# First expert gather from full-precision rows, and four more early weight loads

## Chip, cores and metric

The kernel runs on one core of one Trainium2 chip. The metric is device time in microseconds from one execution; lower is better. The traced execution is one of its own, beside three timed runs.

## What is computed

The reference is one layer of a hybrid encoder trunk on 512 tokens of 1024 channels, float32 in and out:

```python
proj = x @ w_in                       # q,k,v of two attentions, two gate logits
y_sb = stick_breaking(...) @ w_br_sb
y_ca = chunked_relpos(...) @ w_br_ca
mixed = (sigmoid(gl_sb + b0) * y_sb + sigmoid(gl_ca + b1) * y_ca) @ w_out
x = layer_norm(ALPHA * x + mixed, ln1_g, ln1_b)
# router: best of 4 groups, then the best 2 of its 8 experts, with weights
for each expert e: hid = silu(x @ w_gate[e]) * (x @ w_up[e]); y += weight * hid @ w_down[e]
return layer_norm(ALPHA * x + y, ln2_g, ln2_b)
```

The kernel computes an expert only for the tokens that chose it: 32 experts with 64 slots each, two experts to a pair. A dense version behind a branch takes over if an expert overflows; it does not run here.

## The kernel before

**Stages.** Projections and both attentions fill the first 345 us or so. Then comes the output projection `out_proj(half, tt)` (line 748), over two halves of 512 output columns and four token tiles `tt` of 128 rows; VectorE adds its result to the residual rows `hp[tt]` (line 762). With the second half of a tile its first layer norm and its routing follow, spread over the products of later tiles by the table `todo` (lines 1043 to 1053): keys are (half, tile, step), and entries past the last tile are run from `TAIL` (lines 1083 to 1089) together with the first gathers and some filler products that only keep TensorE busy. Then the experts run, `gate_up(e)`, `down(e)`, `act(e)`, in an order written out by hand, and `finish()` adds, normalizes and stores the rows.

**Routing.** `route(tt)` picks group and experts on VectorE; its rank product `rk` (lines 915 to 919) gives each token its slot, from which `slots_of` builds `onehot[:, tt, :]` (lines 928 and 929, 256 columns: the slots of experts 0 to 3). `finish_routing()` makes the row numbers for the rest.

**The first gather.** The tokens of experts 0 to 3 don't come by DMA but by TensorE: for each of the eight channel blocks `c`, `first_x(c, ts)` multiplies 128 columns of the normed rows (stationary) with `onehot[:, tt, :]` (moving) and adds up over the four tiles, through `gathered` (line 995). To do that with fp32r operands the normed rows are split into two parts: `split_h(tt)` (line 837) normalizes `hp[tt]` in two halves on VectorE (line 848), copies each to an fp32r tile `hh` on ACT (line 112), and subtracts it from the row on POOL to get `hl` (line 115). So there are 8 x 4 x 2 = 64 matmuls. Then it stores the rows to DRAM, `hD` (line 853), from where later experts' tokens are fetched with indirect DMA.

**Weights.** An expert's weights come as six chunks of 512 KB, `we0` to `we191`, each loaded by `raw_load()` (line 1063) into a buffer chosen by the table `RING`: `slots` (20 buffers), `slots2` (15), `hip` (4), `lop` (4), 43 in all, used again in turn. `slots2` also holds two gate tiles `gca`, `hp[0..3]`, the rows `lng` and `lnb` of the norm's parameters, and the eight tiles `hh`, `hl`. `load_early` (line 1072) asks for the first 13 chunks at (0,0,5): eight in `slots`, `K2` = 5 in `slots2`. All others are asked for when the experts begin, up to 47 ahead of use, but the queue order is a scheduler's: it issues a load on SP as soon as its buffer is expected to be free, between the stores to `hD`. SP's queue is then fixed, and each entry waits for its own buffer.

Of the kernel before, what the change touches and what calls it, by code (L numbers as in the profile page):

```python
# [9 lines left out]
F32 = mybir.dt.float32  # L10
F32R = mybir.dt.float32r
# [3 lines left out]
AF = mybir.ActivationFunctionType  # L15
OP = mybir.AluOpType
AX = mybir.AxisListType

P = 128
S = 512  # L20
D = 1024
C = D // P
TT = S // P
# [19 lines left out]
WARM = 10  # L43
XEB = 4
AHEAD = 47
EARLY = 13
K2 = 5
EARLY_AT = (0, 0, 5)
NL = 40
PT = (1, 4, 10, 5)  # L50
RA = 2
# [14 lines left out]
IDLE_LAST = 6  # L66

K_POOL = ((0, 1), (0, 2), (0, 3), (1, 0), (1, 1), (1, 2), (1, 3))
H_POOL = (0, 1, 2, 3)
LATE_C = (2, 3)  # L70
H_STT = (0, 1, 2, 3)

LAST_RING = [1 if j % 4 == 1 else 0 for j in range(43)]
RING = [0] * 8 + [1] * K2 + [0] * 12 + [2] * 4 + [3] * 4 + [1] * (NSLOT2 - K2)
SCB = 2
# [28 lines left out]
def trunk(ctx, tc, xT, x, wm, wv, wbr, wout, wr, br, bg, rbx, lnp, lncol, wexp, out):  # L104
    nc = tc.nc
# [3 lines left out]
    def split(hi, lo, src, scale=None, eng=None, fix=False):  # L109

        if scale is None:
            act = nc.scalar.activation(hi, src, AF.Copy)  # L112
            pin(act, fix)
            held[1] = act
            pin((eng or nc.vector).tensor_sub(lo, src, hi.bitcast(F32)), fix == "both")  # L115
        else:
            pin(nc.scalar.activation(hi, src, AF.Copy, scale=scale), fix)
            pin(nc.vector.scalar_tensor_tensor(
                out=lo, in0=src, scalar=scale, in1=hi.bitcast(F32), op0=OP.mult, op1=OP.subtract
            ))  # L120

    in_order = [False]
    held = [None, None]

    def pin(ins, fix=True):
        if in_order[0] and fix:
            tc.keep_in_program_order(ins)

    def mm(ps, a, b, start, stop):
        pin(nc.tensor.matmul(ps, a, b, start=start, stop=stop))  # L130
# [30 lines left out]
    def slot(shape, dtype, name, pool=None):  # L161
        return (pool or slots).tile(shape, dtype, tag="slot", name=name)
# [104 lines left out]
    for cc in range(4):  # L267
        t = slot([P, 2, S], F32, f"xraw{cc}")
        h = slot([P, 2, S], F32R, f"xh{cc}")
        lo = slot([P, 2, S], F32R, f"xl{cc}")  # L270
# [15 lines left out]
    for k in range(4):  # L286
        t = slot([P, 2, S], F32, f"part{k}")
# [8 lines left out]
    for k, pack in enumerate(PACKS[:3]):  # L296
        m = ap_.tile([P, S], BF16, name=f"mask{k}")
        nc.gpsimd.memset(m, 1.0)
        for _, i, off in pack:
            blk = m[:, off + 128 * i : off + 128 * i + 128]  # L300
            nc.gpsimd.affine_select(
                out=blk, in_=blk, pattern=[[-1, P]], compare_op=OP.is_gt, fill=0.0, base=0, channel_multiplier=1
# [160 lines left out]
    def scores(b, p, pack):  # L463
        q, k = QKT["q", b, p], QKT["k", b, p]
        ps = pp.tile([P, S], F32, tag="sc", name="sc", bufs=SCB)
        for h, i, off in pack:
            n = P * (i + 1)
            for z in range(2):
                mm(ps[:, off : off + n], q[:, h, 0, i * P : (i + 1) * P], k[:, h, z, :n], z == 0, z == 1)
        return ps  # L470
# [99 lines left out]
    def run(g, n=1000):  # L570
        if g is None:
            return None
        for _ in range(n):
            try:
                next(g)
            except StopIteration:
                return None
        return g
# [13 lines left out]
    for b in range(2):  # L592
        for p in range(4):
# [6 lines left out]
            for k, pack in enumerate(PACKS):  # L600
# [3 lines left out]
                ps = scores(b, p, pack)  # L604
# [15 lines left out]
    slots2 = es_w.enter_context(tc.tile_pool(name="slots2", bufs=NSLOT2, reuse_waits="tile"))  # L620
# [96 lines left out]
    for t in xgb:  # L717
        nc.gpsimd.memset(t, 0.0)
    onehot = keep.tile([P, TT, 4 * CAP], F32R, name="onehot")
# [17 lines left out]
        out=tri, in_=ones, pattern=[[1, P]], compare_op=OP.is_gt, fill=0.0, base=0, channel_multiplier=-1  # L737
# [6 lines left out]
    hp = [slot([P, D], F32, f"hp{t}", slots2) for t in range(TT)]  # L744
# [83 lines left out]

        return ap.unsqueeze(len(ap.shape)).to_broadcast(list(ap.shape) + [n])

    hh, hl = [None] * TT, [None] * TT
    V = nc.vector

    def centre(tt, mean):
        nc.vector.scalar_tensor_tensor(out=hp[tt], in0=hp[tt], scalar=mean, in1=lng, op0=OP.subtract, op1=OP.mult)

    def split_h(tt):

        r, mean = rs[tt]
        if tt in LATE_C:  # L840
            centre(tt, mean)
        t = slot([P, D], F32R, f"hh{tt}", slots2)
        lo = slot([P, D], F32R, f"hl{tt}", slots2)
        for k in range(2):
            cs = slice(k * S, (k + 1) * S)
            src = hp[tt][:, cs]
            if tt in H_STT:
                nc.vector.scalar_tensor_tensor(out=src, in0=src, scalar=r, in1=lnb[:, cs], op0=OP.mult, op1=OP.add)
            else:
                pin(nc.scalar.activation(src, src, AF.Copy, scale=r))  # L850
                nc.gpsimd.tensor_add(src, src, lnb[:, cs])
            split(t[:, cs], lo[:, cs], src, eng=nc.gpsimd if tt in H_POOL else None, fix=tt in H_STT)
        nc.sync.dma_start(hD[tt * P : (tt + 1) * P, :], hp[tt])
        hh[tt], hl[tt] = t, lo

    NBUF = dict(sc=2, tr=3, pj=2, av=1)
    hqs = [spare.tile([P, 4, P]) for _ in range(2)]
# [23 lines left out]
    def scale1(tt):  # L881
        r, mean = rstd(tail, lnst[tt], TT, None if tt in LATE_C else lambda mean: centre(tt, mean))
        u = small([P, 1], f"u{tt}")
        V.scalar_tensor_tensor(out=u, in0=mean, scalar=-1.0, in1=r, op0=OP.mult, op1=OP.mult)
        rs[tt] = r, mean
        base[tt] = small([P, NL], f"base{tt}")
        V.scalar_tensor_tensor(out=base[tt], in0=swr, scalar=u, in1=brb, op0=OP.mult, op1=OP.add)
        V.scalar_tensor_tensor(out=base[tt], in0=plg[tt][0], scalar=r, in1=base[tt], op0=OP.mult, op1=OP.add)
# [106 lines left out]
    def gathered(ps, c, ts):  # L995

        for tt in ts:
            for n, h in enumerate((hh, hl)):
                mm(
                    ps, h[tt][:, c * P : (c + 1) * P], onehot[:, tt, :],  # L1000
                    tt == 0 and n == 0, tt == TT - 1 and n == 1,
                )

    def xtile(g, j):
        if (g, j) not in xe:
# [5 lines left out]
    def first_x(c, ts):  # L1011

        if len(first) <= c:
            t = (["pj"] * 2 + ["tr"] * 3 + ["av", "sc", "pj"])[c]
            first.append(pp.tile([P, 4 * CAP], F32, tag=t, name="trf", bufs=NBUF[t]))
        gathered(first[c], c, ts)
# [4 lines left out]
    lnb = slot([P, D], F32, "lnb", slots2)  # L1021
# [6 lines left out]
    def turn(tt, q):  # L1028
        lg[tt, q] = logits(tt, q)
        next(lg[tt, q])  # L1030

    def first_half(tt):
        lnst[tt] = stats(tail, hp[tt], 0)

    def begin(tt):
        stats(tail, hp[tt], 1, lnst[tt])

    def choose(tt):
        run(lg[tt, 1])
        rt[tt] = route(tt)  # L1040
        next(rt[tt])

    todo = {}
    for at, half in ((0, 0, 0), 0), ((0, 0, 1), 0), ((0, 0, 3), 0), ((0, 3, 2), 1), ((0, 3, 4), 1), ((0, 3, 6), 1), ((1, 0, 0), 1):
        todo[at] = [lambda half=half: wo[half].append(stream.get())]
    for tt in range(TT):
        at = (0, tt + 1) if tt + 1 < TT else (1, 0)
        todo.setdefault((*at, PT[0]), []).extend([lambda tt=tt: turn(tt, 0), lambda tt=tt: first_half(tt)])
        todo.setdefault((*at, PT[1]), []).append(lambda tt=tt: run(lg[tt, 0]))
        todo.setdefault((1, tt + 1, PT[0]), []).extend([lambda tt=tt: turn(tt, 1), lambda tt=tt: begin(tt), lambda tt=tt: scale1(tt)])  # L1050
        todo.setdefault((1, tt + 1, PT[1]), []).extend([lambda tt=tt: choose(tt)])
        todo.setdefault((1, tt + 1 + PT[2] // 8, PT[2] % 8), []).append(lambda tt=tt: run(rt[tt]))
        todo.setdefault((1, tt + 1 + PT[3] // 8, PT[3] % 8), []).append(lambda tt=tt: split_h(tt))

    seq = []
    for e in range(NE):
# [6 lines left out]
    def raw_load():  # L1063
        i = n_raw[0]
        n_raw[0] += 1
        n = len(RING)
        pool, tag = rooms[RING[i % n] if i < len(seq) - n else LAST_RING[i - len(seq) + n]]
        t = pool.tile([P, D], F32, tag=tag, name=f"we{i}")
        nc.sync.dma_start(t, wexp[seq[i]])
        raw_e.append(t)  # L1070

    def load_early():
        for _ in range(EARLY):
            raw_load()

    todo.setdefault(EARLY_AT, []).append(load_early)
    for half in range(2):
        for tt in range(TT):
            for k, _ in enumerate(out_proj(half, tt)):
# [422 lines left out]
```

## Time and profile before

| | us |
|---|---|
| runs | 679.63, 677.06, 679.90; median 679.63 |
| profiled execution | 682.24, its span 680.4 |
| mean granted TensorE clock | 0.987 |
| PE busy, of the span | 640.9 (94%) |
| DVE busy | 408.2 (60%) |
| ACT busy | 322.6 (47%) |
| POOL busy | 105.1 (15%) |
| DMA moved | 158.62 MB, mean 233 GB/s |

The page of the profile gives busy times by engine, the span in 40 slices of about 17 us, the chain of work that ended last (followed back from the last instruction, at each step to what released it), and the costliest groups of instructions. A row of a timeline has the start, the length, the engine, the line in the kernel, the operation and its tiles; in square brackets stands how long the engine was idle before it and who ended that. "PE" is TensorE, "DVE" VectorE, "ACT" ScalarE, "POOL" GpSimd, "SPq" the queue of SyncE, which issues DMAs. Matmul lengths are modelled with their pipeline, so successive ones overlap, and their rate is read from their starts. A busy PE is not the same as a PE at its peak: fillers count as busy.

### The profile page before, as it was taken

The numbers are of one execution on the slowest core, as the hardware profiler recorded it, in microseconds if no ns is written. First come the engines' busy times: TensorE is split into PE (matmuls) and PEld (weight loads), VectorE is DVE, ScalarE is ACT, GpSimd is POOL, SyncE is SP. The second block draws the span as 40 slices with busy tenths as digits, with TensorE's granted clock in tenths as the row PEclk, the third lists the DMA queues.
The fourth block names the chain that finished last, engine by engine and source line by source line (L and its number), as shares of the span: only waits on it lengthen the run. The fifth ranks groups of instructions, "written<-read, shape, count | busy, mean of one in ns | idle before, by whom it ended". The sixth has DMA issues, their size and how long they took to land.

```text
span 680.4 us, 8940 instructions
## 1 busy us (share of the span) xinstructions
PE 640.9 (94%) x3116; PEld 420.4 (62%) x3116; DVE 408.2 (60%) x836; ACT 322.6 (47%) x642; POOL 105.1 (15%) x152
## 2 busy tenths in 40 slices
PE   8999999999999999989999997899999988889894
PEld 4888878887878888878888775334343322224342
DVE  5676768678868877563674796234444433335466
ACT  5576877766656555744533232333322222222444
POOL 2012121101100110050000133121121111110044
PEclk8999999999999999999999998999999999999997
DMA  8600059203130323016794678999999999999943
GB/s 328 261 0 1 1 191 380 78 2 94 47 108 17 109 78 108 32 57 209 279 362 157 214 252 341 408 408 410 409 408 409 407 408 406 406 403 406 405 198 126
DMA packets 48032, 158.62 MB, mean 233 GB/s; under 512 B 7529, under 2 KB 7673, under 8 KB 47984
## 3 DMA queue, kind: packets, MB, share of 16 engines
q1 hardware_dynamic: 43632, 150.16, 58.2%
q0 software_dynamic: 4352, 7.85, 3.0%
q8 instruction: 26, 0.43, 0.3%
q14 instruction: 22, 0.18, 0.1%
HBM read 150.16 MB, written 15.73 MB: 244 GB/s over the span
## 4 chain that ended last, share of the span: by engine, by line
PE 52%; DMA 20%; DVE 15%; ACT 7%; issue 3%; POOL 0%; SPq 0%; DVEq 0%; POOLq 0%; ACTq 0%
DMA we<-in_wexp_dram 18%; PE pj L130 16%; PE sc L130 10%; PE pb L130 7%; PE po L130 4%; PE tr L130 4%; DVE t L482 3%; PE fin L130 2%; PE pv L130 2%; DVE wl L115 2%; PE av L130 2%; ACT wh L112 2%; DVE t L480 1%; PE tr L536 1%; DMA raw<-in_wm_dram 1%
## 5 line engine op out<-in xcount | busy, mean ns | idle before, releaser
L130 PE MATMUL sc<-we,xp 128*64 128x512 f32 x448 | 108.1, 604 | 7.4 <-DMA we<-in_wexp_dram 5.6
L130 PE MATMUL pj<-xh,wh 128*128 128x512 f32 x256 | 103.9, 406 | 1.7 <-ACT wh L112 1.6
L130 PE MATMUL pj<-xh,wl 128*128 128x512 f32 x256 | 101.2, 395 | 0.0
L130 PE MATMUL pj<-xl,wh 128*128 128x512 f32 x256 | 101.0, 394 | 0.0
L115 DVE TENSOR_TENSOR wl<-raw,wh 128x1024 fp32r<-128x1024 f32 (+1 forms) x57 | 69.9, 1230 | 23.0 <-ACT wh L112 22.8
L1152 DVE TENSOR_TENSOR gus<-gus,sc 64x512 f32<-64x512 f32 x32 | 21.7, 679 | 85.6 <-ACT gus L1151 83.5
L130 PE MATMUL tr<-we,sg 128*64 128x512 f32 x256 | 63.3, 601 | 5.3 <-DMA we<-in_wexp_dram 2.6
L112 ACT ACTIVATE wh<-raw 128x1024 fp32r<-128x1024 f32 (+1 forms) x57 | 58.7, 1037 | 18.7 <-DMA raw<-in_wbr_dram 4.7
L130 PEld LDWEIGHTS sc<-we,xp 128*64 128x64 f32 x448 | 27.4, 136 | 63.2 <-issue 33.1
L1151 ACT ACTIVATE gus<-sc 64x512 f32<-64x512 f32 x32 | 19.0, 593 | 88.6 <-PE sc L130 88.6
L130 PEld LDWEIGHTS pj<-xh,wh 128*128 128x128 f32 x256 | 48.6, 190 | 11.2 <-ACT wh L112 2.1
L130 PEld LDWEIGHTS pj<-xh,wl 128*128 128x128 f32 x256 | 48.5, 189 | 11.1 <-DVE wl L115 0.4
L130 PEld LDWEIGHTS pj<-xl,wh 128*128 128x128 f32 x256 | 48.6, 190 | 8.4
L130 PEld LDWEIGHTS tr<-we,sg 128*64 128x64 f32 x256 | 16.4, 136 | 44.9 <-issue 31.5
L130 PE MATMUL pb<-y,wh 128*128 128x512 f32 x128 | 40.0, 394 | 0.3 <-DVE k L345 0.3
L115 DVE TENSOR_TENSOR wl<-tr,wh 128x512 fp32r<-128x512 f32 (+1 forms) x64 | 30.9, 484 | 11.9 <-ACT wh L112 11.6
L1225 POOL DMA_INDIRECT y2D<-oe,rowi x14 | 14.0, 998 | 146.3 <-DVE oe L1216 120.2
L489 POOL TENSOR_SCALAR_AFFINE_SELECT w<-w 128x128 f32<-128x128 f32 x32 | 16.1, 514 | 126.2 <-ACT w L486 118.5
L112 ACT ACTIVATE wh<-tr 128x512 fp32r<-128x512 f32 (+1 forms) x64 | 27.2, 427 | 12.7 <-PE tr L536 12.4
L1214 ACT ACTIVATE oe<-tr,wswap 64x512 f32<-64x512 f32 x28 | 19.1, 682 | 26.0 <-DVE oe L1218 25.7
L130 PE MATMUL sc<-k,q 128*128 128x512 f32 (+3 forms) x128 | 28.5, 323 | 0.2
L1218 DVE SCALAR_TENSOR_TENSOR oe<-tr,wslot,xg 64x512 f32<-64x512 f32 x24 | 18.0, 750 | 17.0 <-PE tr L130 17.0
(229 smaller groups left out, 1218.9 us busy)
## 6 DMA issues: line engine op xcount, KB each, us to landing
we<-in_wexp_dram SPq DMA_DIRECT2D x192, 512.0 KB
raw<-in_wm_dram SPq DMA_DIRECT2D x32, 512.0 KB
raw<-in_wv_dram SPq DMA_DIRECT2D x8, 512.0 KB
y2D<-zero SPq DMA_DIRECT2D x16, 256.0 KB
raw<-in_wbr_dram SPq DMA_DIRECT2D x8, 512.0 KB
raw<-in_wout_dram SPq DMA_DIRECT2D x8, 512.0 KB
yy<-y2D SPq DMA_DIRECT2D x8, 512.0 KB
strip<-in_rbx_dram SPq DMA_DIRECT2D x8, 256.0 KB
```

Of the source, the lines that this page charges most:

```text
L112: act = nc.scalar.activation(hi, src, AF.Copy)
L115: pin((eng or nc.vector).tensor_sub(lo, src, hi.bitcast(F32)), fix == "both")
L130: pin(nc.tensor.matmul(ps, a, b, start=start, stop=stop))
L480: nc.vector.scalar_tensor_tensor(out=t, in0=ps, scalar=0.0, in1=t, op0=OP.max, op1=OP.add)
L482: nc.vector.tensor_tensor_scan(out=t[:, ::-1], data0=t[:, ::-1], data1=mk[:, ::-1], initial=0.0, op0=OP.add, op1=OP.mult)
L489: nc.gpsimd.affine_select(out=blk, in_=blk, pattern=[[-1, P]], compare_op=OP.is_gt, fill=0.0, base=0, channel_multiplier=1)
L536: nc.tensor.transpose(tr[:, i * P : (i + 1) * P], w[:, off + j * P : off + (j + 1) * P], ident)
L1151: pin(nc.scalar.activation(gus[e], ps[CAP:], AF.Copy))
L1152: pin(nc.vector.tensor_add(gus[e], gus[e], ps[:CAP]))
L1214: nc.scalar.activation(dst, ps[here], AF.Copy, scale=(wslot if half == odd else wswap)[here, p : p + 1])
L1218: nc.vector.scalar_tensor_tensor(out=dst, in0=ps[here], scalar=wslot[here, p : p + 1], in1=xg[p][here, cs], op0=OP.mult, op1=OP.add)
L1225: nc.gpsimd.indirect_dma_start(out=y2D[:, :], out_offset=bass.IndirectOffsetOnAxis(ap=rowi[:, p : p + 1], axis=0), in_=oe[p], in_offset=No ...
```

## The change

The split goes. `split_h` becomes `norm_h`: the same two VectorE instructions per tile and the same store, without the copies and subtractions. `gathered` takes `hp[tt]` itself as the stationary operand and reads `onehot` as float32, so that one product in full precision stands where two fp32r ones stood; the profile records a full-precision product as two matmuls. The eight buffers of `hh` and `hl` aren't taken any more. `EARLY` becomes (13, 4): the first 13 chunks are asked for where they were, and four more at (0,3,5); `K2` becomes 9, so that `RING` has nine places of `slots2` behind the first eight, and six instead of ten at its end. It still has 43.

```diff
-EARLY = 13
-K2 = 5
-EARLY_AT = (0, 0, 5)
+EARLY = (13, 4)
+K2 = 9
+EARLY_AT = ((0, 0, 5), (0, 3, 5))
...
 RING = [0] * 8 + [1] * K2 + [0] * 12 + [2] * 4 + [3] * 4 + [1] * (NSLOT2 - K2)
...
-    def split_h(tt):
+    def norm_h(tt):
 
         r, mean = rs[tt]
         if tt in LATE_C:
             centre(tt, mean)
-        t = slot([P, D], F32R, f"hh{tt}", slots2)
-        lo = slot([P, D], F32R, f"hl{tt}", slots2)
         for k in range(2):
             cs = slice(k * S, (k + 1) * S)
             src = hp[tt][:, cs]
-            if tt in H_STT:
-                nc.vector.scalar_tensor_tensor(out=src, in0=src, scalar=r, in1=lnb[:, cs], op0=OP.mult, op1=OP.add)
-            else:
-                pin(nc.scalar.activation(src, src, AF.Copy, scale=r))
-                nc.gpsimd.tensor_add(src, src, lnb[:, cs])
-            split(t[:, cs], lo[:, cs], src, eng=nc.gpsimd if tt in H_POOL else None, fix=tt in H_STT)
+            held[1] = nc.vector.scalar_tensor_tensor(
+                out=src, in0=src, scalar=r, in1=lnb[:, cs], op0=OP.mult, op1=OP.add
+            )
         nc.sync.dma_start(hD[tt * P : (tt + 1) * P, :], hp[tt])
-        hh[tt], hl[tt] = t, lo
...
         for tt in ts:
-            for n, h in enumerate((hh, hl)):
-                mm(
-                    ps, h[tt][:, c * P : (c + 1) * P], onehot[:, tt, :],
-                    tt == 0 and n == 0, tt == TT - 1 and n == 1,
-                )
+            mm(ps, hp[tt][:, c * P : (c + 1) * P], onehot[:, tt, :].bitcast(F32), tt == 0, tt == TT - 1)
...
-    def load_early():
-        for _ in range(EARLY):
+    def load_early(n):
+        for _ in range(n):
             raw_load()
 
-    todo.setdefault(EARLY_AT, []).append(load_early)
+    for at, n in zip(EARLY_AT, EARLY):
+        todo.setdefault(at, []).append(lambda n=n: load_early(n))
```

## Rows read from the trace of the kernel before

**Rows 1.** The page: DMA busy tenths and GB/s in 40 slices

```profile
DMA  8600059203130323016794678999999999999943
GB/s 328 261 0 1 1 191 380 78 2 94 47 108 17 109 78 108 32 57 209 279 362 157 214 252 341 408 408 410 409 408 409 407 408 406 406 403 406 405 198 126
```

**Rows 2.** Chain that ended last, in order of time: start, us, what

```profile
518.44 12.01 DMA we<-in_wexp_dram
...
643.35 5.71 DMA yy<-y2D
```

**Rows 3.** Busy time by stretch: stretch, its length, engines' us, PEclk, DMA share, GB/s

```profile
360.00:368.00 8.00, 8.00 (x45) 6.64 (x44) 2.55 (x4) 2.35 (x4) 0.00 (x0) 1.00 0.14 55
392.00:396.00 4.00, 4.00 (x23) 3.08 (x22) 4.00 (x11) 1.23 (x2) 2.61 (x2) 1.00 0.43 105
409.00:411.00 2.00, 0.41 (x4) 0.20 (x2) 2.00 (x6) 0.57 (x1) 0.84 (x1) 0.88 0.21 86
411.00:412.00 1.00, 1.00 (x5) 1.00 (x6) 0.97 (x3) 0.26 (x2) 0.86 (x1) 0.50 0.78 311
412.00:416.00 4.00, 4.00 (x29) 3.96 (x27) 3.88 (x20) 0.42 (x2) 2.36 (x10) 0.76 0.97 301
416.00:420.00 4.00, 3.11 (x26) 2.88 (x24) 3.10 (x9) 1.53 (x4) 1.17 (x4) 1.00 1.02 416
420.00:424.00 4.00, 3.73 (x18) 1.06 (x16) 0.42 (x1) 0.19 (x1) 0.00 (x0) 1.00 1.03 413
```

**Rows 4.** Timeline of SP's queue: start, us, queue, line, what is issued

```profile
352.44 1.61 SPq L178 DMA_DIRECT2D raw<-in_wout_dram  x2
...
410.42 0.33 SPq L853 DMA_DIRECT2D hD<-hp  x1
410.79 4.08 SPq L1069 DMA_DIRECT2D we<-in_wexp_dram  x7
...
419.34 0.33 SPq L1069 DMA_DIRECT2D we<-in_wexp_dram  x1
...
425.54 0.33 SPq L1069 DMA_DIRECT2D we<-in_wexp_dram  x1
...
435.78 0.33 SPq L1069 DMA_DIRECT2D we<-in_wexp_dram  x1
```

**Rows 5.** What SP's queue waited for, 403 to 412 us: total, times, longest

```profile
SPq L853 <- DVE hp L848: 6.0, 1, 6.0
```

**Rows 6.** Timelines of ACT, PE, DVE and POOL around the fourth tile's norm

```profile
371.82 1.06 ACT L112 ACTIVATE wh<-raw 128x1024 fp32r<-128x1024 f32 x1 [0.33 <-PE po L130]
...
400.53 0.39 PE L130 MATMUL po<-wh,ml 128*128 128x512 f32 x1
...
402.30 0.66 DVE L762 SCALAR_TENSOR_TENSOR hp<-hp,po 128x512 f32<-128x512 f32 x1
...
406.94 0.74 DVE L848 SCALAR_TENSOR_TENSOR hp<-hp,small_xe,lnb 128x512 f32<-128x512 f32 x1
...
408.71 1.68 DVE L848 SCALAR_TENSOR_TENSOR hp<-hp,small_xe,lnb 128x512 f32<-128x512 f32 x1
...
408.48 1.36 POOL L115 TENSOR_TENSOR hl<-hp,hh 128x512 fp32r<-128x512 f32 x1 [4.63 <-ACT hh L112]
```

**Rows 7.** Timeline of TensorE: end of the gather, an expert's down product, final addition

```profile
415.17 0.19 PE L130 MATMUL rk<-small_oe,small_xe 128*128 128x32 bf16 x1
...
417.28 0.36 PE L130 MATMUL trf<-onehot,hh 128*128 128x256 f32 x1 [0.89 <-DVE onehot L929]
417.48 0.28 PE L130 MATMUL trf<-onehot,hl 128*128 128x256 f32 x1
...
419.87 0.28 PE L130 MATMUL trf<-onehot,hl 128*128 128x256 f32 x1
...
432.64 1.94 PE L130 MATMUL tr<-we,sg 128*64 128x512 f32 x8
...
655.32 3.60 PE L130 MATMUL fin<-yy,ident 128*128 128x512 f32 x8
```

More of the change, by code (lines that the diff above doesn't have):

```diff
@@ L68 @@
 K_POOL = ((0, 1), (0, 2), (0, 3), (1, 0), (1, 1), (1, 2), (1, 3))
-H_POOL = (0, 1, 2, 3)
 LATE_C = (2, 3)
-H_STT = (0, 1, 2, 3)
 LAST_RING = [1 if j % 4 == 1 else 0 for j in range(43)]
@@ L829, in last @@
         return ap.unsqueeze(len(ap.shape)).to_broadcast(list(ap.shape) + [n])
-    hh, hl = [None] * TT, [None] * TT
     V = nc.vector
@@ L1052, in trunk @@
         todo.setdefault((1, tt + 1 + PT[2] // 8, PT[2] % 8), []).append(lambda tt=tt: run(rt[tt]))
-        todo.setdefault((1, tt + 1 + PT[3] // 8, PT[3] % 8), []).append(lambda tt=tt: split_h(tt))
+        todo.setdefault((1, tt + 1 + PT[3] // 8, PT[3] % 8), []).append(lambda tt=tt: norm_h(tt))
     seq = []
```

## Prediction

> **What bounds the kernel now.** I read the page first. In the second half of the span the DMA row stands at nines and the GB/s row near 408, while the first half has holes [rows 1]. So I went to the chain that ended last: from 518.4 us on it is made of loads of expert weights (`we`), and at 643.4 us it passes to the loads of the routed rows [rows 2]. From there to the end the kernel waits for one stream of 192 loads of 512 KB. At 413 GB/s [rows 3] a load takes 524.3 KB / 413 = 1.27 us. The stream is dense from 412 us, so its end moves only if work is taken out of it, or if idle DMA time before that is filled. The windows show idle time in two places that matter: 360 to 368 us, where the DMA share is 0.14 (8 x 0.86 = 6.9 us idle), and 409 to 411 us, where it is 0.21 (1.6 us idle) [rows 3].
>
> What starts the loads comes next. SP issues them one after the other in the order of its queue, each when its buffer is free. The first hole lies behind the last two loads of output-projection weights, issued at 352.4 us [rows 4]; what follows them in the queue has no free buffer yet. The second is another matter: SP waited 6.0 us for line 848 before it could issue the last store of normed rows, at 410.42 us, and the seven loads behind it start only then [rows 4, 5].
>
> **The change part by part.** (1) Four loads move. The eight buffers of the split parts are gone, nine chunks can stand in `slots2` beside the four `hp`, `lng` and `lnb`, and the four added loads come at (0,3,5), so SP finds them right behind the two loads of 352.4 us. Their traffic ran until about 361 us (360 plus 0.14 x 8); four more take 4 x 1.27 = 5.1 us and end near 366 us, inside the hole [rows 3]. Nothing urgent is behind them: if they went ahead of the last output-projection chunk instead, it would land 5.1 us later, near 366 us, and the last split of such a chunk starts at 371.8 us [rows 6]. Cost beneath that cover: nothing; without it up to 5.1 us of TensorE. Gain at the end of the stream: 5.1 us.
>
> (2) The split goes: 8 ACT copies and 8 POOL subtractions at line 115. POOL's took VectorE with them. The same scalar_tensor_tensor of line 848 takes 0.74 us alone and 1.68 us when a subtraction runs on POOL beside it [rows 6], 0.94 us more, and the last tile's second half waits behind it.
>
> TensorE's last output projection begins at 400.53 and lasts 0.39 us, but VectorE evacuates it only at 402.30 us [rows 6]: up to 1.4 us of backlog goes as well. So the last store can leave at about 410.4 - 0.9 - 1.4 = 408.1 us, before DMA ran dry at about 409.4 us (409 plus 0.21 x 2) [rows 3]. The second hole closes: 1.6 us. Bounds: 0, if VectorE is held up elsewhere, and 3.0 us, if an earlier store also falls into a hole that ends at its issue (392 to 396 us has a share of 0.43, 2.3 us idle) [rows 3]. I take 1.6 us, since that hole has its own wait shown.
>
> (3) The price is on TensorE. One product of 256 columns is now two fp32r matmuls that follow each other at 0.12 us (417.48 to 419.87 us, 21 starts), 0.24 us in all [rows 7]. In full precision the nearest row is the final addition: 4 products of 512 columns, 8 records (two per product) in 3.60 us, so at most 3.60 / 8 = 0.45 us each, and a little less since the last record's length is in it; I take 0.43. For 256 columns that is half of 2 x 0.43 = 0.43 us. The gather's 32 products cost 32 x 0.19 = 6.1 us more. From both sides: 0 more, if a second record were free, and 32 x (0.86 - 0.24) = 19.8 us, if TensorE stood at its lower clock, half of the other, throughout. The page FP8 and Floating Point Precision of the Trainium skill, "TensorE Precision Notes", counts four passes for a true FP32 product, and that speaks against this change. Four passes of the 0.12 us row would be 0.48 us a product, +7.7 us in all and 0.6 us later at the gather's end than reckoned below, which would leave 0.2 us of the cover found there and speaks for rival (a); no row of this trace shows the gather itself in that form.
>
> Most of that price lies where TensorE fills time before the fourth tile's one-hot. What lies on a path is the end: about 11 products follow the last one-hot at 417.28 us and end at 420.0 us [rows 7]; they become 11 x 0.43 = 4.7 us instead of 2.7, +2.0 us. Ahead of it, the fourth tile's rank product at 415.17 us stands behind six products and 12 fillers, run from about 411 us at the 1.2 GHz level (granted clock 0.50 at 411) after TensorE had been busy for 0.41 of 2 us [rows 3, 7]. With VectorE earlier by some 2 us, those six take 2.6 us at 2.4 GHz or 5.2 us at 1.2 GHz. I bound the rank product by 412 and 418 us and take 414 us, near its row. Then 2.1 us to the one-hot, as now (415.17 to 417.28), and 4.7 us: the gather ends at 420.8 us, between 418.8 and 424.8 us.
>
> **What that end decides** is when the four `hp` come free. Loads up to the 35th (before) or 39th (after) need no buffer that the gather reads; the next waits for it, all later weight loads stand behind that one in SP's queue, and TensorE's experts wait for those. Before, the 36th was issued at 419.34 us [rows 4], yet DMA still had work: eight transfers (the store at 410.42 us and the seven loads after it [rows 4]) are 4194 KB; 311 + 4 x 301 + 4 x 416 = 3179 KB had moved by 420.0 us, and the rest at 413 GB/s lasts until 422.5 us [rows 3]. After, the same eight lie in front, 1.6 us earlier: DMA would run dry at 420.9 us. A load needs 0.6 us from its issue (410.42) to traffic (411.0), and the first `hp` is free three products, 1.3 us, before the gather's end. So the end may slip to 420.9 - 0.6 + 1.3 = 421.6 us without cost. My 420.8 us lies just inside. This cover is thin: 0.8 us; each further us costs one.
>
> **Sum.** 5.1 + 1.6 - 0 = 6.7 us. The profiled execution took 682.24 us (span 680.4); it becomes 675.5 us. The median of the runs, 679.63 us, is 2.6 us lower, and the same gain gives 672.9 us.
>
> **The rivals.** (a) The gather ends late, at 424.8 us: it is 3.2 us past the cover, the gain shrinks to 3.5 us: 676.1 us. For it: the low clock at 411 us. Against: VectorE's earlier one-hots leave TensorE less idle.
>
> (b) The loads come early but DMA idles later, since the ring of 43 buffers is full. The 52nd load needs the 9th chunk, whose product starts at 432.64 us, so about 433.6 us; it was issued at 435.78 us [rows 4, 7] and would be wanted 6.7 us earlier, at 429.1 us. It would be 4.5 us late, but loads queue: the 44th, eight places ahead and issued at 425.54 us, starts moving at 422.5 + 8 x 1.27 = 432.7 us, 7.2 us after issue. The queue covers 4.5 us. The same end follows if the four loads don't start before 368 us, held by buffers: the change would then not do what it says. Either way the gain is 0 to 2 us: 679 us.
>
> (c) Stores also fill earlier holes, up to 3.0 us instead of 1.6, and the output projection's two short waits go: gain 8 to 9 us, 671 us.
>
> (d) Slower: the whole gather at 1.2 GHz. The 11 products then take 9.5 us, the six 5.2 us, and the fillers stretch: it ends at 424.8 + 4.8 = 429.6 us, and with a rank product at 420 us at 431.6. It loses from 421.6 + 6.7 = 428.3 us on: 1.3 to 3.3 us lost, 681 to 683 us. Against: the clock was back at 1.00 at 416 us [rows 3], and the longer products keep TensorE busier.
>
> **How the numbers follow.** Forecast 672.9 us: 0.50. (a) 676.1 us, from 675 to 678: 0.22. (b) 679 us: 0.10. (c) 671 us: 0.11. (d) 682 us: 0.07. Within 0.5% (3.4 us, about what a measurement of this kernel can tell from no change) lie (b), a third of (a), and a third of (d): 0.10 + 0.07 + 0.02 = 0.19. Slower by more: 0.05. Faster by more: 0.76. The range takes the forecast, (c) and (a) with its bound: 670.0 to 678.0 us.
>
> **What would show it.** DMA share near 1.0 from 360 to about 366 us; no hole near 410 us; line 848's successor at 0.75 us each; 64 records of the gather on `hp`, 0.21 us apart; DMA without a gap from 404 us on; the first wait of TensorE for a weight load later than 518 us. I am wrong if DMA idles between 415 and 425 us (gather late), if 360 to 368 us is still empty, or if loads after the 43rd wait for buffers with DMA idle.

## The result, and the profile after

| | before | after |
|---|---|---|
| median of six runs, us | 679.76 | 673.20 |
| lowest to highest, us | 677.06 to 681.91 | 670.35 to 673.85 |
| ratio, 95% interval | | 0.9873 (0.9836 to 0.9911) |
| profiled execution (span), us | 682.24 (680.4) | 673.75 (672.0) |

The kernel is faster by 1.3%; 672.9 us was forecast. The profiled execution fell by 8.49 us where the sum said 6.7. The page of the profile after, the rows that answer to [rows 1]:

```profile
DMA  8600049203130315014797669999999999999953
GB/s 327 268 0 1 1 168 389 83 19 95 48 109 18 111 25 164 24 50 135 303 350 309 220 228 391 392 408 408 410 408 405 407 407 404 408 408 400 410 201 128
```

The 22nd slice (from 353 us) rose from 157 to 309 GB/s and the 25th (from 403 us) from 341 to 391. The windows show where, in the columns of [rows 3]:

```profile
360.00:368.00 8.00, 8.00 (x44) 6.65 (x44) 2.02 (x3) 2.35 (x4) 0.00 (x0) 1.00 0.68 272
...
392.00:396.00 4.00, 4.00 (x23) 3.13 (x22) 3.59 (x16) 0.98 (x3) 0.00 (x0) 1.00 0.54 164
...
409.00:411.00 2.00, 2.00 (x14) 1.84 (x14) 1.87 (x9) 0.21 (x1) 1.89 (x9) 1.00 0.93 301
411.00:412.00 1.00, 1.00 (x10) 0.96 (x10) 0.22 (x1) 0.00 (x0) 0.43 (x3) 1.00 1.07 389
412.00:416.00 4.00, 4.00 (x22) 3.41 (x21) 2.62 (x8) 1.03 (x3) 0.59 (x2) 1.00 1.02 411
...
420.00:424.00 4.00, 2.57 (x16) 0.88 (x14) 0.68 (x1) 2.08 (x3) 0.00 (x0) 1.00 0.93 330
```

The DMA share of 360 to 368 us went from 0.14 to 0.68, and of 409 to 411 us from 0.21 to 0.93: the second hole has closed, and the first has taken what the four loads bring. The granted clock is 1.00 in each row, where it had fallen to 0.50 at 411 us. New is the last row: 330 GB/s instead of 413. SP's queue, as in [rows 4]. First two stores of before that aren't among those rows, then the queue after:

```profile
393.89 0.33 SPq L853 DMA_DIRECT2D hD<-hp  x1
...
401.86 0.33 SPq L853 DMA_DIRECT2D hD<-hp  x1
```

```profile
349.97 2.09 SPq L176 DMA_DIRECT2D raw<-in_wout_dram  x2
352.95 26.18 SPq L1056 DMA_DIRECT2D we<-in_wexp_dram  x10
...
392.73 0.38 SPq L845 DMA_DIRECT2D hD<-hp  x1
...
399.79 0.37 SPq L845 DMA_DIRECT2D hD<-hp  x1
...
406.57 0.33 SPq L845 DMA_DIRECT2D hD<-hp  x1
```

The early loads begin at 352.95 us, right behind the last two of the output projection's weights. The last store leaves at 406.57 instead of 410.42 us. What SP waited for between 403 and 440 us answers to [rows 5]:

```profile
SPq L1056 <- PE trf L128: 6.2, 2, 5.3
SPq L845 <- DVE hp L842: 3.9, 1, 3.9
```

The longest wait is now for the gather (`trf`), that of the 40th load. TensorE's and VectorE's rows, as in [rows 6, 7]:

```profile
399.17 0.39 PE L128 MATMUL po<-wh,ml 128*128 128x512 f32 x1
...
411.54 0.19 PE L128 MATMUL rk<-small_oe,small_xe 128*128 128x32 bf16 x1
...
412.37 5.86 PE L128 MATMUL trf<-onehot,hp 128*128 128x256 f32 x26
```

VectorE's evacuation of the last product, and the second half of that tile's norm:

```profile
399.59 0.69 DVE L760 SCALAR_TENSOR_TENSOR hp<-hp,po 128x512 f32<-128x512 f32 x1
...
405.82 0.73 DVE L842 SCALAR_TENSOR_TENSOR hp<-hp,small_xe,lnb 128x512 f32<-128x512 f32 x1
```

Line 842, the successor of line 848, takes 0.73 us here, and the gather ends at 412.37 + 5.86 = 418.2 us. The chain that ended last now passes from TensorE to the weight loads at 561 us, where it did so at 518 us before [rows 2]:

```profile
559.51 1.75 PE sc L128 x7
561.26 11.22 DMA we<-in_wexp_dram
...
638.86 4.94 DMA yy<-y2D
```

### The profile page after: what moved, and what is told of

The parts are those of the page before. It is cut to its first block, busy times and chain, and to the rows that moved or that the text cites. A ratio compares the mean times of both kernels' runs of the same rounds, so it can differ in the third digit from the quotient of the medians.

```text
span 672.0 us, 8914 instructions
## 1 busy us (share of the span) xinstructions
PE 641.8 (95%) x3116; PEld 423.5 (63%) x3116; DVE 402.5 (60%) x836; ACT 317.3 (47%) x634; POOL 94.2 (14%) x144
## 4 chain that ended last, share of the span: by engine, by line
PE 67%; DVE 11%; DMA 10%; ACT 7%; issue 3%; POOL 0%; SPq 0%; DVEq 0%; POOLq 0%; ACTq 0%
PE pj L128 16%; PE sc L128 15%; DMA we<-in_wexp_dram 8%; PE po L128 7%; PE pb L128 7%; PE tr L128 6%; DVE t L480 3%; PE trf L128 3%; PE fin L128 3%; DVE wl L113 3%; PE pv L128 3%; PE av L128 2%; ACT wh L110 2%; PE pj L1113 2%; DMA raw<-in_wm_dram 2%
## 5 line engine op out<-in xcount | busy, mean ns | idle before, releaser
L128 PE MATMUL sc<-we,xp 128*64 128x512 f32 x448 | 106.3, 602 | 3.5 <-DMA we<-in_wexp_dram 2.2
L534 PE MATMUL tr<-ident,w 128*128 128x128 f32 x160 | 27.8, 272 | 0.0
```

The lines of the kernel that those rows point to most:

```text
L534: nc.tensor.transpose(tr[:, i * P : (i + 1) * P], w[:, off + j * P : off + (j + 1) * P], ident)
```

## The experiments

Two theories stood against each other. **Stream**: the end is set by the stream of weight loads, so what counts is idle DMA time filled, by the four loads and by earlier stores. **Routing**: what counts is VectorE freed of the split and the experts' earlier start, and the four loads are hidden anyway.

The first 345 us, whose code no kernel here changes, vary more between executions than most effects: the first output-projection product, at 345.41 us before, lies between 343 and 352 us. So positions in the profiled executions are counted from that product: to TensorE's first expert product, to the load of routed rows behind the weight stream (before 640.83 - 345.41 = 295.42), and to the end of the span.

| kernel | median, us | ratio (95%) | experts start | stream ends | span ends |
|---|---|---|---|---|---|
| before | | | 74.67 | 295.42 | 335.02 |
| after | 673.20 | 0.9873 (0.9836 to 0.9911) | 72.85 | 287.19 | 326.73 |
| a0_change_again | 673.12 | 0.9883 (0.9838 to 0.9928) | 72.81 | 287.46 | 327.00 |
| e1_no_loads | 677.92 | 0.9986 (0.9957 to 1.0015) | 72.84 | 292.02 | 331.45 |
| e2_split_kept | 675.33 | 0.9935 (0.9909 to 0.9961) | 76.35 | 290.68 | 330.17 |
| e3_late_before | 681.09 | 1.0033 (1.0002 to 1.0063) | 76.82 | 296.20 | 335.71 |
| e4_late_after | 673.97 | 0.9914 (0.9892 to 0.9935) | 75.82 | 289.56 | 329.24 |
| e5_no_fill | 672.51 | 0.9865 (0.9827 to 0.9903) | 71.62 | 287.20 | 326.70 |
| e6_late_experts | 674.20 | 0.9889 (0.9839 to 0.9938) | 75.94 | 289.75 | 329.33 |
| e7_no_fill_at_all | 672.97 | 0.9895 (0.9845 to 0.9944) | 71.65 | 287.30 | 327.04 |
| e8_copies_only | 671.93 | 0.988 (0.9813 to 0.9947) | 72.89 | 287.76 | 327.34 |
| e9_pool_memset | 671.26 | 0.987 (0.9792 to 0.9949) | 72.82 | 287.69 | 327.30 |

The ratios are against before on the same chip: 679.86 us beside e1 to e4, 681.4 us beside a0 and e5 to e7, 679.81 us beside e8 and e9. Each position is from one execution. From the stream's end to the end of the span it is 39.4 to 39.7 us in every row, so the last column follows from the one ahead of it. Four kernels that differ in nothing that should move the stream (after, a0, e8, e9) have it end at 287.19 to 287.76: positions alone tell apart no less than 0.6 us.

Where the stream gains or loses can be read from the traces themselves, in stretches counted from the same product: 0 to 24 us holds the first hole, 46 to 72 us the second and the smaller ones ahead of it, 72 to 84 us the wait for the gather. In before, then in after:

```profile
345.41:369.41 24.00, 24.00 (x124) 19.98 (x123) 11.09 (x21) 7.01 (x16) 0.00 (x0) 1.00 0.64 249
391.41:417.41 26.00, 21.75 (x136) 18.78 (x136) 25.77 (x91) 6.39 (x15) 11.14 (x18) 0.93 0.77 263
417.41:429.41 12.00, 10.57 (x61) 5.24 (x61) 3.12 (x8) 3.84 (x8) 0.00 (x0) 1.00 1.03 413
```

```profile
345.31:369.31 24.00, 24.00 (x124) 19.98 (x123) 11.09 (x21) 7.01 (x16) 0.00 (x0) 1.00 0.86 336
391.31:417.31 26.00, 26.00 (x151) 22.49 (x150) 21.80 (x92) 4.13 (x13) 2.91 (x12) 1.00 0.86 322
417.31:429.31 12.00, 9.85 (x49) 4.02 (x47) 2.91 (x8) 2.77 (x5) 0.00 (x0) 1.00 0.98 376
```

The DMA time that a stretch leaves unused, against 413 GB/s, is its length times (1 - GB/s / 413): 24 x (1 - 249/413) = 9.5 us in the first row. For the runs of the argument, with 84 to 100 us as a fourth stretch, and what the sum says the stream gains on before beside what its position says (sums from unrounded values):

| kernel | 0 to 24 | 46 to 72 | 72 to 84 | 84 to 100 | gain by the sum | gain by position |
|---|---|---|---|---|---|---|
| before | 9.5 | 9.4 | 0.0 | 0.2 | | |
| after | 4.5 | 5.7 | 1.1 | 0.2 | 7.8 | 8.2 |
| e1_no_loads | 9.3 | 6.2 | 0.2 | 0.2 | 3.3 | 3.4 |
| e2_split_kept | 4.1 | 9.4 | 0.7 | 0.1 | 4.9 | 4.7 |
| e4_late_after | 4.4 | 5.9 | 2.8 | 0.2 | 6.0 | 5.9 |
| e5_no_fill | 4.4 | 6.6 | 0.0 | 0.3 | 8.0 | 8.2 |
| e6_late_experts | 4.3 | 6.1 | 0.5 | 2.6 | 5.7 | 5.7 |

So the stream's end moves by the idle DMA time that is filled or left, within 0.5 us in every row.

**The change once more**, on the chip of e5 to e7, with nothing edited.

> The changed kernel itself, beside the others on one chip. Counted from the first product of the output projection, the stream's end and the end of the span lie 8.2 to 8.3 us before those of the kernel before in the trace of the change; the runs' medians say 6.6 us. Stream theory: 8 us again from that point, and 671 to 674 us; about 1 us of DMA idle time between 418 and 424 us.

Its median is 8.3 us under that of before, against 6.6 us at first; by position the stream ends 7.96 us earlier, against 8.23.

**The change without its four loads.**

```diff
-NSLOT2 = 15
+NSLOT2 = 11
...
-EARLY = (13, 4)
-K2 = 9
-EARLY_AT = ((0, 0, 5), (0, 3, 5))
+EARLY = (13,)
+K2 = 5
+EARLY_AT = ((0, 0, 5),)
```

> The change without its four loads: the split is gone and the gather reads the rows in full precision, but `slots2` has 11 buffers instead of 15, so the four freed buffers aren't used and 13 chunks are early, as before. Stream theory (the end is the end of the weight stream, so the gain is the DMA idle time that is filled): the hole at 360 to 368 us stays, that near 410 us closes; of the 8.3 us by which the stream's end moved in the trace of the change, 5.1 us are missing: 2 to 3.5 us faster than before, about 677 us. Routing theory (the gain comes from the shorter routing and the earlier start of the experts, 418.2 instead of 420.1 us, and VectorE no longer held up): nearly all of it stays, 671 to 674 us.

The experts start as early as in the whole change (72.84), yet the median falls by only 1.9 us (0.9957 to 1.0015: between 2.9 us faster and 1.0 us slower) and the stream ends 3.4 us earlier, not 8.2. The hole stays open, here counted 6 us later because the first part was longer:

```profile
366.00:374.00 8.00, 8.00 (x45) 6.65 (x44) 2.01 (x4) 2.23 (x4) 0.00 (x0) 1.00 0.05 22
415.00:417.00 2.00, 2.00 (x13) 1.82 (x12) 1.98 (x10) 0.21 (x1) 1.59 (x7) 1.00 0.93 272
```

The second row is the hole of 409 to 411 us, closed without the loads. The routing theory, which gave the loads nothing and expected 671 to 674 us here, falls.

**The change with the split kept beside it.** The copies and subtractions run, into a buffer that is free at that time; nobody reads them, and the gather stays in full precision.

```diff
+            split(xgb[0][:, cs].bitcast(F32R), xgb[1][:, cs].bitcast(F32R), src, eng=nc.gpsimd, fix=True)
         nc.sync.dma_start(hD[tt * P : (tt + 1) * P, :], hp[tt])
```

> The change with the split's work put back: ACT copies and POOL subtracts as before, into two tiles (`xg`) that nobody reads before they are written anew; the gather reads the full-precision rows, the four loads are early. Stream theory: 5.1 us of loads in the hole at 360 to 368 us stay, but VectorE is held up by POOL again, the last store leaves about 2 us later, the hole near 410 us opens again and the gather ends later than DMA can wait: 2 to 5 us faster than before, 675 to 678 us. Routing theory: no gain, 679 to 681 us, since the experts start later than before.

Experts start 1.7 us later than before the change, and still the stream ends 4.7 us earlier and the median is 4.5 us lower: that is what the loads are worth alone, less what the late experts cost. The windows of the two holes:

```profile
358.00:366.00 8.00, 8.00 (x45) 6.64 (x44) 2.19 (x3) 2.47 (x5) 0.00 (x0) 1.00 0.70 280
407.00:409.00 2.00, 1.51 (x12) 1.05 (x12) 1.99 (x6) 0.66 (x2) 0.70 (x1) 1.00 0.19 78
```

The first is filled, the second is back (0.19, before 0.21). By positions the two parts add up: 3.4 + 4.7 = 8.1, the whole change 8.2. The medians can't check that: 1.9 + 4.5 = 6.4 stands against 6.6 once and 8.3 in a0.

How the split holds VectorE is seen by laying its rows in this kernel against POOL's:

```profile
397.93 1.70 DVE L842 SCALAR_TENSOR_TENSOR hp<-hp,small_xe,lnb 128x512 f32<-128x512 f32 x1
...
400.68 1.04 DVE L891 TENSOR_TENSOR small_xe<-small_xe 128x4 f32<-128x4 f32 x1
```

```profile
397.64 1.43 POOL L113 TENSOR_TENSOR xg<-hp,xg 128x512 fp32r<-128x512 f32 x1 [3.95 <-ACT xg L110]
400.42 1.27 POOL L113 TENSOR_TENSOR xg<-hp,xg 128x512 fp32r<-128x512 f32 x1 [1.35 <-ACT xg L110]
```

Line 891 handles four elements a partition and takes 0.15 us where POOL is idle. Here it ends at 401.72 us, just after POOL at 401.69. Both of VectorE's instructions began while POOL subtracted, and ended about as if their work had begun when POOL was done (0.1 to 0.2 us sooner). An instruction with two inputs of which one (`plg`) lies in PSUM, the matmuls' result memory, isn't held. In before it ran in the midst of a subtraction and took the 0.26 us that it takes without one:

```profile
384.23 0.26 DVE L894 SCALAR_TENSOR_TENSOR small_oe<-plg,small_xe 128x40 f32<-128x40 f32 x1
```

```profile
383.87 1.42 POOL L115 TENSOR_TENSOR hl<-hp,hh 128x512 fp32r<-128x512 f32 x1 [79.27 <-ACT hh L112]
```

**Copies alone; then POOL instructions that only write.** Which part of the split does it?

```diff
+            nc.scalar.activation(xgb[0][:, cs], src, AF.Copy)
```

> The changed kernel with the 8 ACT copies of the split put back, into a tile that nobody reads, and no subtractions. Where the run with the whole split's work lost 3.5 us of the change's gain (counted from the first product of the output projection), this asks which part. If POOL's subtractions hold VectorE up: nothing is lost, the stream's end lies within 0.4 us of the change's (287.2 to 287.5 us from that point), line 842 takes 0.74 us each. If it is ACT's copies (its queue, or the row tiles read once more): up to 3.5 us lost.

```diff
+            nc.scalar.activation(xgb[1][:, cs], src, AF.Copy)
+            nc.gpsimd.memset(xgb[1][:, cs], 0.0)
+            nc.gpsimd.memset(xgb[1][:, cs], 0.0)
```

> The changed kernel with the 8 copies and, behind each, two POOL memsets of 128 x 512 on the copied tile, which nobody reads: POOL is busy at the same places but reads no memory. If VectorE is held up by any work of POOL: line 842 and its neighbours take up to 1.7 us again and up to 3.5 us of the gain are lost. If it is held up only where POOL reads the same memory side: 0.74 us each, nothing lost.

The group of line 842 (count, then minimum, median and maximum in ns, first and last start) in e8:

```profile
L842 DVE SCALAR_TENSOR_TENSOR hp<-hp,small_xe,lnb x8: 732/742/747, 380.3 to 403.8; 128x512 f32<-128x512 f32 x8
```

The same in e9:

```profile
L842 DVE SCALAR_TENSOR_TENSOR hp<-hp,small_xe,lnb x8: 727/744/746, 380.4 to 404.3; 128x512 f32<-128x512 f32 x8
```

And in e2:

```profile
L842 DVE SCALAR_TENSOR_TENSOR hp<-hp,small_xe,lnb x8: 745/747/1697, 380.1 to 406.6; 128x512 f32<-128x512 f32 x8
```

Neither ACT's copies nor POOL's 16 memsets (0.53 us each) lengthen these instructions, although the memsets do fall on them: the line 842 of 389.40 to 390.14 us in e9 had memsets beside it from 389.09 to 390.20 us, with a pause of 0.06 us. Both kernels stand by position with the whole change (they were run twice each, so their ratios say little). It is POOL's subtraction, which reads two tiles, that holds VectorE's instructions with two inputs in SBUF. The Trainium skill says so, in SBUF — State Buffer, "Who interferes with whom": a VectorE instruction with two SBUF inputs gets the second through a read interface shared with GpSimd, so it collides with a GpSimd instruction that reads SBUF, not with one that only writes it. This case's 1.70 against 0.74 us, the 0.26 us of line 894, and e9 agree.

**A later gather, in before and in after.** 32 fillers instead of 6 ahead of the last products.

```diff
-IDLE_LAST = 6
+IDLE_LAST = 32
```

> The kernel before with 26 more filler products (256 columns, 0.12 us each, 3.1 us) ahead of the last part of the gather. Stream theory: when the 36th load's buffer comes free DMA still has about 3 us of work, less 0.6 us to start: the end moves by 0 to 0.7 us. Routing theory: the experts start 3.1 us later, and so does the end: 3.1 us slower.

> The changed kernel with the same 26 fillers (3.1 us). Stream theory: the four chunks that were moved ahead have used up the cover, the 40th load waits for the gather with DMA nearly out of work, so the end moves by about 3 us: against before only 4 to 5 us faster, with DMA idle near 420 us. If the cover is still there: 0 to 1 us. Routing theory: 3.1 us.

In before, experts 2.15 us later cost 0.8 us of the stream: cover was there, some 1.4 us of it (2.15 - 0.78). In after, experts 2.97 us later cost 2.4 us of the stream. By the median, e4 is only 0.8 us above after and still 5.9 us under before, where 4 to 5 was expected; such a difference is within the scatter of the first part. DMA runs dry in e4 at the place where after was only thin:

```profile
416.00:418.00 2.00, 2.00 (x11) 1.74 (x10) 0.21 (x1) 0.38 (x1) 0.00 (x0) 1.00 0.22 88
418.00:420.00 2.00, 2.00 (x10) 0.83 (x10) 0.42 (x1) 0.00 (x0) 0.00 (x0) 1.00 0.64 203
```

**Gather as in after, experts later.** 26 fillers behind the gather, so that `hp` comes free on time and only the ring's buffers are late.

```diff
     prep_first()
+    in_order[0] = True
+    for _ in range(26):
+        mm(first[NFIRST - 1], zr, onehot[:, 2, :], True, True)
+    in_order[0] = False
```

> The changed kernel with 26 fillers (3.1 us) behind the gather's last product, ahead of the first expert: the gather's buffers come free as in the change, but the chunks of the first experts are used up 3.1 us later. If the time lost near 420 us and in the run with fillers ahead of the gather comes from the rows' buffers alone: 0 to 0.5 us slower than the change. If the ring of 43 buffers binds as well (the 44th load needs the first chunk): 1.5 to 2.5 us slower, with DMA idle between 420 and 432 us.

The experts start 3.1 us later and the stream ends 2.6 us later (the median is 1.1 us above a0's). DMA is still full where e4 ran dry and loses its time 10 us further on:

```profile
418.00:420.00 2.00, 2.00 (x19) 2.00 (x18) 0.42 (x1) 0.00 (x0) 0.00 (x0) 1.00 1.02 408
...
431.00:433.00 2.00, 0.74 (x4) 0.59 (x4) 1.17 (x6) 0.70 (x5) 0.65 (x1) 1.00 0.99 317
```

So there are two covers, and both are nearly used up: of the gather's delay all but 0.6 us is paid (2.97 - 2.37, e4), of the experts' delay all but 0.5 us (3.09 - 2.56, e6). The first is the rows' buffers up to the gather's end, the second the ring up to the experts' first chunks. Both remainders are no more than positions can tell apart.

**An earlier gather.** Without the 18 fillers ahead of the fourth tile; then without any.

```diff
-IDLE = {(1, 4, 4): 6, (1, 4, 5): 12}
+IDLE = {}
```

> The changed kernel without the 6 and 12 filler products that stand between the gather's parts ahead of the fourth tile's rank product (1.8 us of TensorE stand directly ahead of it); the 6 of the end stay. Stream theory: the rank product, the gather's end and the experts come 1.0 to 1.8 us earlier, DMA no longer idles near 420 us, and the end moves by what was lost there, 1.0 us, so 0.5 to 1.1 us faster than the change. If TensorE's clock falls for want of work, the gather ends later: 0 to 2 us slower than the change. If the hole near 420 us is the ring's and not the gather's, the gain is the same, since the experts move too.

```diff
-IDLE = {(1, 4, 4): 6, (1, 4, 5): 12}
-IDLE_LAST = 6
+IDLE = {}
+IDLE_LAST = 0
```

> As the run without the fillers ahead of the rank product, and the six behind it go too, which stand where TensorE waits for the fourth one-hot. Stream theory: no further gain, within 0.5 us of that run, since products of the gather fill that wait and DMA no longer waits for it. If the clock falls: up to 2 us slower.

Both start the experts 1.2 us earlier, and the thin stretch fills; in e5:

```profile
416.00:418.00 2.00, 2.00 (x12) 0.62 (x10) 0.00 (x0) 0.00 (x0) 0.00 (x0) 1.00 1.03 416
418.00:420.00 2.00, 0.98 (x6) 0.10 (x2) 0.32 (x1) 0.93 (x2) 0.00 (x0) 1.00 1.04 422
```

But the stream ends at 287.20 and 287.30, as in after (287.19), and the medians differ from a0's by 0.6 and 0.2 us. The table of unused DMA time says where it went: in e5 the stretch from 72 to 84 us is full (0.0 instead of 1.1 us), but 46 to 72 us leaves 6.6 instead of 5.7 us. Within that lie two slow microseconds, in which DMA was busy and moved little:

```profile
407.00:409.00 2.00, 2.00 (x14) 1.75 (x13) 1.98 (x11) 0.21 (x1) 1.49 (x7) 1.00 1.01 193
```

What slowed it there is open. So the earlier gather does close the thin stretch, and the expected 0.5 to 1.1 us at the end did not come. No version here is shown to beat the change.

## Why the prediction was right, point by point

**The stream sets the end: right.** From the stream's end everything keeps its distance of 39.4 to 39.7 us, and the end doesn't follow the experts' start: in e2 the experts start 1.7 us later than in before and the span ends 4.9 us earlier.

**Four loads, 5.1 us: right.** They went where they were expected: the first hole's stretch leaves 5.1 us less unused (9.5 to 4.5), and e2, with the second hole open, gains 4.7 us by position and 4.5 us by median. Rival (b), loads held by buffers or by the ring, fell with the 0.68 of 360 to 368 us.

**The split, 1.6 us: right mechanism, mis-sized term.** The second hole closed, but the stretch around it gave 3.7 us (9.4 to 5.7), and 3.3 us in e1, both beyond the term's upper bound of 3.0. By the median e1 gave 1.9 us, with an interval that ends at 2.9; its single runs scatter from 675.2 to 684.8 us, more than the term. Four things were left out of the sum:

- The hole was read by its DMA share of 0.21, so it ended at 411 us. But [rows 3] has 311 GB/s from 411 to 412 and 301 from 412 to 416 us, at shares of 0.78 and 0.97: 0.25 + 1.08 = 1.3 us more unused DMA time behind it. In after these five microseconds move 389 and 411 GB/s.

- POOL held more than line 848. The four-element instruction beside it (line 899 of before) waited too, and so did line 901, with 32 elements; their groups in before, with the columns of line 842's:

```profile
L899 DVE TENSOR_TENSOR small_xe<-small_xe x4: 164/516/996, 385.0 to 411.0; 128x4 f32<-128x4 f32 x4
L901 DVE SCALAR_TENSOR_TENSOR small_xe<-small_xe,small_oe x4: 169/712/1286, 385.3 to 411.2; 128x32 f32<-128x32 f32 x4
```

  In after they take 0.15 to 0.16 and 0.14 to 0.19 us. I had charged 0.94 us a tile, and it was up to 0.94 + 0.84; in the fourth tile line 901 waited 1.1 us, behind the last store but ahead of the rank product.
- TensorE's output projection became 1.26 us shorter: 345.31 to 399.17, from 345.41 to 400.53 us. 0.73 us of that were idle; the two short waits that rival (c) named come and go with the split, and the other 0.5 us I can't place. TensorE's waits in before, in that stretch (total, times, longest):

```profile
PE trh L865 <- DVE hp L762: 0.4, 1, 0.4
PE rk L130 <- DVE small_oe L912: 0.2, 1, 0.2
```

In after there are none; its window has TensorE busy throughout (54.00 of 54.00 us):

```profile
345.30:399.30 54.00, 54.00 (x282) 44.72 (x282) 35.33 (x96) 12.87 (x30) 0.00 (x0) 1.00 0.74 274
```

In e2, with the split kept, they are back:

```profile
PE trh L857 <- DVE hp L760: 0.4, 1, 0.4
PE rk L128 <- DVE small_oe L904: 0.3, 1, 0.3
```

- So the last store left 3.85 us earlier where 2.3 were reckoned: 1.36 from the output projection's end (0.10 of it from its start), 1.35 from the backlog between it and its evacuation (402.30 - 400.53 = 1.77, now 399.59 - 399.17 = 0.42), 0.94 from line 848, 0.2 not placed. The two stores ahead of it moved by 1.2 and 2.1 us and filled part of earlier holes (392 to 396 us: 0.43 to 0.54). These were rival (c)'s pieces; I gave it 0.11, and by position (8.2 us) its gain is what happened.

**The price on TensorE: right in size, wrong in place.** The 26 records on `hp` from 412.37 us start 0.22 us apart, so a product takes 0.43 us, as taken. But the rank product came at 411.54 us, ahead of its lower bound of 412. VectorE, which had waited 0.87 us for it, had the one-hot ready at 413.15 us, 1.6 us later, and TensorE didn't wait for that: products of earlier tiles had begun at 412.37 us. The gather ended at 418.2 us where 420.8 was forecast and 418.8 the early bound. Rivals (a) and (d) rested on the clock of 0.50 at 411 us [rows 3]; it stayed at 1.00 up to 424 us, with TensorE busy in all of 409 to 420 us.

**"Inside the cover, cost nothing": this step failed, by 1.1 us.** The cover was reckoned from the moment at which DMA would run dry, 1.6 us earlier than before, at 420.9 us. The last store left 3.85 us earlier, and the queue did run short sooner: from 368.6 us, where it was empty, the 22 loads and four stores up to the 39th load are 26 x 524.3 KB = 13.6 MB, and at the 273 GB/s that DMA moved on average from there they were through at about 419 us. With that moment the prediction's own rule would still allow the gather to end at 419 - 0.6 + 1.3 = 419.7 us, and it ended at 418.2. Yet from 417.31 to 429.31 us DMA moved 376 instead of 413 GB/s, 1.1 us lost. So it is the rule that failed, which takes DMA as full up to the last byte and full again 0.6 us after the next load's issue: SP waited 5.3 us for the gather, no load was issued in that time, and with the queue nearly empty DMA thinned out to 330 GB/s (the row of 420 to 424 us above) instead of stopping and starting. e4 bears it out, with 2.8 us lost there for a gather 2.97 us later, and e5, where the stretch is full. That the end of the stream would come earlier for it was not shown (e5, e7).

The sum with the measured sizes: 5.1 for the loads, 3.7 for the split, 1.1 lost at 420 us: 7.7, where the positions of after, a0, e8 and e9 say 7.7 to 8.2 and the medians 6.6 and 8.3. The forecast of 6.7 was near in part by luck: a gain 2.1 us too small and a cost of 1.1 us put at nothing stood against each other.

## What to carry to other kernels

Where one dense stream of loads sets the end, price a change by the idle DMA time ahead of the stream that it fills, hole by hole, and look for the wait that ends each hole. Read a hole by the GB/s of the rows behind it and not by the DMA share alone. A gain in the stream also moves the moment at which its covers run out, so reckon the cover with the gain already in it. When an instruction is taken off an engine that holds up another, look through all of the neighbour's rows in that stretch for lengthened ones, small ones too, and not at the longest alone.

## What the runs showed of the hardware

- A POOL subtraction of two tiles delays VectorE's instructions with two SBUF inputs that start beside it for about the rest of its run, whatever their size: 0.74 to 1.70 us for 128x512, 0.19 to 1.29 us for 128x32, 0.15 to 1.04 us for 128x4. One with an input in PSUM is not delayed (0.26 us), and POOL memsets beside line 842 do nothing (727 to 746 ns).
- A full-precision product with 256 moving columns is recorded as two matmuls, 0.22 us apart, 0.43 us together, against 0.12 us for one fp32r product: 3.6 times as much. The four passes that the Trainium skill counts for true FP32 (FP8 and Floating Point Precision, "TensorE Precision Notes") would make 0.48 us, by estimate from the 0.12 us; the measured value is a little lower.
- A high DMA share doesn't say that DMA moves at its full rate: 0.97 at 301 GB/s (before, 412 to 416 us), 0.93 at 330 (after, 420 to 424 us), 1.01 at 193 (e5, 407 to 409 us), against 1.03 at 413. So GB/s has to be read beside the share.
